# The residual of a down projection, joined after the first block instead of before it

## The chip, the cores and the metric

The kernel runs on one core of one Trainium2 chip. The metric is the device time of one execution in microseconds (us), as the median of three runs. The engines are named as in the profile: PE is TensorE (matmuls) and PEld its weight loads, DVE is VectorE, ACT is ScalarE, POOL is GpSimd, and SP is the engine whose queue issues the DMAs.

## The reference

One decoder layer: a mixer of two kinds of attention, cross-attention, and a multilayer perceptron, each added to a residual. Only the last part matters here. With x the residual of 1024 tokens by 1024 features:

```
u = relu(rmsnorm(x, ln2) @ w_ff1)        # 1024 -> 4096
x = x + (u * u) @ w_ff2                  # 4096 -> 1024: the down projection
return rmsnorm(x, ln_f)
```

All arithmetic is float32. The kernel writes each operand of a matmul as the sum of a rounded high part and the low rest, and takes three matmuls (low x high, high x low, high x high) for each product.

## The kernel before, in words

The activations lie with features on the 128 partitions and tokens along the free dimension, in two halves of 512 tokens.

**The recipe of seven.** Both projections of the perceptron are cut into blocks, and a block is a product of 2 x 2 by 2 x 2 sub-blocks done with seven products in place of eight (the Strassen-Winograd recipe). The inner dimension of 4096 makes eight blocks of 512 (`NB = 8`). Blocks 0 to 6 of the down projection use the recipe; block 7 is done plainly by `last_part` (L1559).

**The up projection** (the loop at L1422) works on 16 pairs `p_` of row tiles, two for each block. `Pair.run` (L1328) does one product of a pair (12 matmuls of 128x128 by 128x512) and evicts it. With a pair's last product (4) its results u11, u12, u21, u22 are complete, and `put_right` (blocks 0 to 6) or `put_plain` (L1393, block 7) makes a list of closures, `later`. Each closure writes tiles to DRAM with `put` (L1362): ACT copies a tile to its rounded high part in a small buffer (tags d and e), DVE makes the low part in place, and two DMAs of 256 KB write both. One closure is taken from `later` ahead of each product (L1433); what is left after the last product is run at L1441. Those are seven closures, all of `put_plain`, for block 7. Its order within a pair was u11, u21, u12, u22.

**The weights of the down projection.** `left(src)` (L1400) loads 512 KB of weights for one step into a buffer `wr` (two of these), lets POOL make four sums of quarters (L1410, tile z), and splits twice: the plain quarters into two tiles of the tag w4 (hq, lq: products 1, 2 and 4) and the sums into wh and wl (three buffers each: products 5, 6, 7 and 3). In the profile the high parts are ACT's line L132 and the low parts DVE's line L133. The tag w4 has five buffers. In the transition they are shared by hq and lq of the steps, by the tile that holds u22 of a pair, and by `by_norms`.

**The right operands** of a block are seven tiles of 1 MB (`rights`, L1446), loaded from DRAM into large tiles of the tag act. There are seven of these; four serve a block's right operands, and two are the running sums `x2`.

**The residual.** The kernel carries the down projection's sums divided by a norm factor for each token (`by_norms`, a row of 1024 repeated on all partitions, in a w4 buffer). The residual is in DRAM as `x2d`. Before, `x2_load(m)` (L1456) loads it for one of four row groups m, 1 MB, straight into the tile of the running sums; `scaled(m)` (L1469) multiplies it by `by_norms`, two DVE operations of 128x1024; and `distances` (L1475) lets POOL subtract the quarter x22 from x12 and x21. For, in the recipe, x12 and x21 are kept as their distance from x22, and `distances` with an addition at block 6 undoes it.

**The steps** (the loop at L1481) go over blocks b = 0 to 6 and, in each, row groups m = 0 to 3. A step asks for the next step's weights, then issues the loads that are to stand behind these in SP's queue (`issue_after`): the residual's next row group in the first three steps, and the next block's right operands in steps m = 2 and 3. Then come the seven products in the order 1, 5, 7, 6, 2, 4, 3, of six matmuls each. Products 2, 4 and 3 go on in the PSUM banks of products 1, 5 and 7. After each product a DVE operation adds the bank to a running sum or subtracts it (L1507): products 1, 5, 7 and 6 in turn to x22, then 2 to x11, 4 to x21 and 3 to x12. Products 2, 4 and 3 need the bank read before they begin.

**Order.** Each engine executes its queue in order. The kernel is written with a scheduler that places each engine's instructions by a timeline of its own, from the order of the program as a priority and from what is ready; so the order in the profile isn't quite that of the program. For example, products of step 1 whose weights were ready stand ahead of late products of step 0.

Of the kernel before, what the change touches and what calls it, by code (L numbers as in the profile page):

```python
# [11 lines left out]
AF = mybir.ActivationFunctionType  # L12
ALU = mybir.AluOpType
# [6 lines left out]
TH = 512  # L20
# [24 lines left out]
def hybrid_layer(ctx: ExitStack, tc: tile.TileContext, a: dict, out: bass.AP):  # L45
    nc = tc.nc
    v, s, g = nc.vector, nc.scalar, nc.gpsimd
# [11 lines left out]
    def sb(tag, shape, bufs, dt=F32):  # L59
        return pool.tile(shape, dt, tag=tag, name=name(tag), bufs=bufs)  # L60

    def act(dt=F32R):
        return sb("act", [P, 8, TH], 7, dt)
# [8 lines left out]
    def w4(shape=(P, 1024), dt=F32):  # L72
        t = sb("w4", [P, 1024], 5, dt)[: shape[0]]
        return t.rearrange("p (a b) -> p a b", b=shape[2]) if len(shape) == 3 else t
# [4 lines left out]
    def w2(tag, n=512, dt=F32, p=P):  # L79
        return sb("r_" + tag, [P, 512], BUFS[tag], dt)[:p, :n]  # L80
# [15 lines left out]
    def ov_():  # L96
        return ps_tile("ov")
# [13 lines left out]
    load = nc.sync.dma_start  # L111
# [70 lines left out]
    def mm3(ps, w, x, first, last, more=False):  # L182

        nc.tensor.matmul(ps, w[1], x[0], start=first, stop=False, skip_group_check=more)  # L184
        nc.tensor.matmul(ps, w[0], x[1], start=False, stop=False, skip_group_check=more)  # L185
        nc.tensor.matmul(ps, w[0], x[0], start=False, stop=last, skip_group_check=more)  # L186

    def both(pair, f):
        return f(pair[0]), f(pair[1])
# [76 lines left out]
    at = 0  # L266
# [33 lines left out]
    h = [(act(), act()), (act(), act())]  # L300
# [20 lines left out]
    for k in range(KT):  # L321
        if k == 2:
            load(wg_raw, a["w_gate"])
        if k % 2 == 0:
            c = slice(k % 4 * 256, k % 4 * 256 + 512)
# [93 lines left out]
    ps = ov_()  # L419
# [260 lines left out]
    for _ in range(2):  # L680
        t = act().rearrange("p a b -> p (a b)").rearrange("p (i c) -> p i c", i=4)
# [455 lines left out]
    x2d = dram.tile([P, KT // 2, 2, 2, TH], F32, name="x2d")  # L1137
# [23 lines left out]
    def bank():  # L1161
        turn[0] += 1
        return ps_tile(cycle[turn[0] % 8])

    def sub(out_, x, y, by=v):
        by.tensor_tensor(out=out_, in0=x, in1=y, op=ALU.subtract)
# [195 lines left out]
    def put(dst, x):  # L1362

        hi = rotate("d", "e").bitcast(F32R)
        split(hi, x.bitcast(F32R), x)
        load(dst[0], hi.bitcast(F32))
        load(dst[1], x)
# [24 lines left out]

    def put_plain(k, pair):  # L1393
        f = lambda i, hf: lambda: put([plain[2 * i + k, :, p_, hf] for p_ in range(2)], pair.u[f"{i + 1}{hf + 1}"])
        return [f(i, hf) for hf in range(2) for i in range(2)]


    after = [None]

    def left(src):  # L1400

        q = sb("wr", [P, 1024], 2)
        after[0] = load(q, src)
        q = q.rearrange("p (q c) -> p q c", q=4)
        q21, q11, q12, q22 = (q[:, i] for i in range(4))
        sums = z4()[:, :1024].rearrange("p (q c) -> p q c", q=4)
        s1, s2, s3, s4 = (sums[:, i] for i in range(4))

        for o, x, y, op in ((s1, q21, q22, ALU.add), (s2, s1, q11, ALU.subtract), (s3, q11, q21, ALU.subtract), (s4, s2, q12, ALU.subtract)):
            g.tensor_tensor(out=o, in0=x, in1=y, op=op)  # L1410
        hq, lq = (w4(dt=F32R)[:, :768].rearrange("p (q c) -> p q c", q=3) for _ in range(2))
        split(hq, lq, q[:, 1:])
        hs, ls = (sb(t, [P, 1024], 3, F32R).rearrange("p (q c) -> p q c", q=4) for t in ("wh", "wl"))
        split(hs, ls, sums)
        f = lambda hi, lo, i: both((hi, lo), lambda t: t[:, i].rearrange("p (k c) -> p k c", k=2))
        return {1: f(hq, lq, 0), 2: f(hq, lq, 1), 3: f(hs, ls, 3), 4: f(hq, lq, 2), 5: f(hs, ls, 0), 6: f(hs, ls, 1), 7: f(hs, ls, 2)}

    by_norms = w4()

    pairs = {}  # L1420
    later = []
    for at, (p_, i) in enumerate(jobs):  # L1422
        prepare(at)
        for _ in range(2 if at < 2 else 1):
            if rest and at:
                rest.pop(0)()
        if at == 6:
            norm_factors(1)
        if at == 30:
            to_row(by_norms, inv, 8, rowd[3:4], bank)  # L1430
        if at == len(jobs) - 3:
            lefts = left(a["w_ff2q"][0, 0])
        if later:  # L1433
            later.pop(0)()
        pair = pairs.setdefault(p_, Pair(p_))
        pair.run(i, cuts.pop((p_, i)))
        if i == 4:
            b, k = todo[p_][:2]
            later += put_right(b, k, pair) if b < NB - 1 else put_plain(k, pair)
            del pairs[p_]  # L1440
    for f in later:  # L1441
        f()

    SEVEN = (1, 5, 7, 6, 2, 4, 3)

    def rights(b, at):  # L1446

        t = act()
        n = min(2, 7 - at)
        for e in range(n):  # L1450
            load(t[:, 4 * e : 4 * e + 4].bitcast(F32), right[b][at + e].rearrange("p e k c -> p (e k) c"))
        return {SEVEN[at + e]: (t[:, 4 * e : 4 * e + 2], t[:, 4 * e + 2 : 4 * e + 4]) for e in range(n)}

    x2 = []

    def x2_load(m):  # L1456
        if m % 2 == 0:
            x2.append(act(F32).rearrange("p (m i h) c -> p m i h c", m=2, i=2))
        load(x2[m // 2][:, m % 2], x2d[:, m])

    steps = [(b, m) for b in range(NB - 1) for m in range(4)]
    r = {}
    r.update(rights(0, 0))
    r.update(rights(0, 2))
    x2_load(0)
    r.update(rights(0, 4))
    r.update(rights(0, 6))

    def scaled(m):  # L1469

        for i in range(2):
            x = x2[m // 2][:, m % 2, i].rearrange("p h c -> p (h c)")
            v.tensor_tensor(out=x, in0=x, in1=by_norms, op=ALU.mult)

    def distances(op, m):  # L1475

        x = x2[m // 2][:, m % 2]
        for i, hf in ((0, 1), (1, 0)):
            g.tensor_tensor(out=x[:, i, hf], in0=x[:, i, hf], in1=x[:, 1, 1], op=op)

    for at, (b, m) in enumerate(steps):  # L1481
        now = lefts
        if m == 0:
            r_now, r = r, {}
        if at + 1 < len(steps):
            b1, m1 = steps[at + 1]
            lefts = left(a["w_ff2q"][b1, m1])
        with tc.issue_after(after[0].ins):
            if at < 3:
                x2_load(at + 1)  # L1490
            if b + 1 < NB - 1:
                for i in ((), (), (0,), (2, 4, 6))[m]:
                    r.update(rights(b + 1, i))
        if at == 0:
            scaled(0)
            distances(ALU.subtract, 0)
        x = x2[m // 2][:, m % 2]
        x11, x12, x21, x22 = (x[:, i, j] for i in range(2) for j in range(2))
        held = {}

        for i, of, y, op in ((1, 1, x22, ALU.add), (5, 5, x22, ALU.add), (7, 7, x22, ALU.add), (6, 6, x22, ALU.add), (2, 1, x11, ALU.add), (4, 5, x21, ALU.subtract), (3, 7, x12, ALU.subtract)):
            if of == i:
                held[of] = bank()
            ps = held[of]
            for k in range(2):
                mm3(ps, both(now[i], lambda t: t[:, k]), both(r_now[i], lambda t: t[:, k]), of == i and k == 0, k == 1, True)
            v.tensor_tensor(out=y, in0=y, in1=ps, op=op)  # L1507
            if at < 3 and i == 5:
                scaled(at + 1)
                distances(ALU.subtract, at + 1)  # L1510
        if b == NB - 2:
            distances(ALU.add, m)


    us = []
    for i in range(2):
        t = act()
# [123 lines left out]
```

## Time and profile before

| | |
|---|---|
| median of three runs | 1542.23 us (1541.98 to 1542.44) |
| the profiled execution's own time | 1540.44 us |
| its span, from first to last instruction | 1538.7 us |
| granted TensorE clock, mean | 0.997 |
| down projection with the recipe | from about 1194 us, its last eviction starts at 1482.0 us |
| residual loads (L1459), four of 1 MB | issued from 1180.8 to 1215.0 us |
| scalings (L1473) | from 1189.4 to 1226.3 us |

Times within the profile are from the start of the span. A row of a group or of the timeline names the engine, the line, the operation, and "out<-in" by the program's tiles (the names of PSUM tiles are those of their tags: sc, tp, ov, and mm, m for the two single banks; tags such as r_d are the small buffers, wr, wh, wl, w and z those of the weights, with w for w4). "x" and a number is a count; "[idle before <-releaser]" tells how long the engine stood idle and whose end released it. A row of waits reads: who waited, for whom, in total us, how often, the longest.

### The profile page before, as it was taken

The page shows a single profiled execution, that of the slowest core. Times are in us where ns is not written, and L with a number is a line of the kernel's source. Part 1 is how long each engine was busy: PE and PEld are TensorE (multiplying, and loading weights), DVE is VectorE, ACT ScalarE, POOL GpSimd, SP SyncE. Part 2 cuts the span into 40 slices and gives each one's busy share as a digit, 9 for nine tenths or more (in the row PEclk, how much of TensorE's full clock was granted, in tenths as well). Part 3 has the DMA queues.
Part 4 walks back from the last instruction along what each step waited for, and adds up shares of the span by engine and source line. Part 5 has one row for each costly group of instructions (what it writes and reads, how often), then busy time and mean ns, then how long its engine had stood idle before and what let it go on. Part 6 is the DMA issues. An engine that isn't in the chain of part 4 may idle for free. (4 is left out here: it accounts for less than half of the span.)

```text
span 1538.7 us, 22030 instructions
## 1 busy us (share of the span) xinstructions
PE 1509.2 (98%) x7729; PEld 1259.7 (82%) x7729; DVE 1123.0 (73%) x1724; ACT 722.9 (47%) x1349; POOL 489.9 (32%) x527
## 2 busy tenths in 40 slices
PE   8999999999999999999999999999999999999997
PEld 8878888889898887788888877778787688888887
DVE  7656676665788875854457889898887987767665
ACT  7324343334688763543443466666664421111224
POOL 0002130414455441521110024544545543333322
PEclk9999999999999999999999999999999999999998
DMA  6422223436887958953444437776678966666623
GB/s 222 122 79 83 91 102 122 131 127 163 249 246 225 305 178 287 314 185 117 137 141 142 162 130 281 246 253 240 219 253 299 355 262 246 245 240 242 244 96 110
DMA packets 119803, 303.54 MB, mean 197 GB/s; under 512 B 13310, under 2 KB 27960, under 8 KB 111756
## 3 DMA queue, kind: packets, MB, share of 16 engines
q1 hardware_dynamic: 119692, 302.13, 57.7%
q8 instruction: 61, 1.00, 0.3%
q14 instruction: 50, 0.41, 0.1%
HBM read 202.22 MB, written 99.86 MB: 196 GB/s over the span
## 5 line engine op out<-in xcount | busy, mean ns | idle before, releaser
L184 PE MATMUL tp<-act,wl 128*128 128x512 f32 (+1 forms) x448 | 176.2, 393 | 1.4 <-ACT row L1339 0.7
L185 PE MATMUL tp<-act,wh 128*128 128x512 f32 (+1 forms) x448 | 175.3, 391 | 0.0
L186 PE MATMUL tp<-act,wh 128*128 128x512 f32 (+1 forms) x448 | 174.7, 391 | 0.0
L133 DVE TENSOR_TENSOR wl<-wr,wh 128x1024 fp32r<-128x1024 f32 (+2 forms) x99 | 129.5, 1309 | 23.7 <-ACT wh L132 23.4
L132 ACT ACTIVATE wh<-wr 128x1024 fp32r<-128x1024 f32 (+2 forms) x99 | 99.0, 1000 | 87.7 <-PE tp L186 34.6
L184 PE MATMUL mm<-act,wl 128*128 128x512 f32 (+1 forms) x336 | 130.6, 389 | 1.8 <-DVE r_c L518 0.9
L186 PE MATMUL mm<-act,wh 128*128 128x512 f32 (+1 forms) x336 | 129.0, 384 | 0.0
L185 PE MATMUL mm<-act,wh 128*128 128x512 f32 (+1 forms) x336 | 128.8, 383 | 0.0
L184 PE MATMUL m<-act,wl 128*128 128x512 f32 (+1 forms) x312 | 120.6, 386 | 2.0 <-POOL wl L947 1.6
L186 PE MATMUL m<-act,wh 128*128 128x512 f32 (+1 forms) x312 | 119.3, 382 | 0.0
L185 PE MATMUL m<-act,wh 128*128 128x512 f32 (+1 forms) x312 | 119.1, 382 | 0.0
L184 PEld LDWEIGHTS tp<-act,wl 128*128 128x128 f32 x448 | 84.2, 188 | 21.8 <-DVE wl L133 1.7
L1410 POOL TENSOR_TENSOR z<-wr 128x256 f32<-128x256 f32 x56 | 52.1, 950 | 152.1 <-DMA wr<-w_ff2q 139.2
L186 PEld LDWEIGHTS tp<-act,wh 128*128 128x128 f32 x448 | 84.2, 188 | 19.2
L185 PEld LDWEIGHTS tp<-act,wh 128*128 128x128 f32 x448 | 84.2, 188 | 18.8
L184 PE MATMUL sc<-act,wl 128*128 128x512 f32 (+1 forms) x248 | 97.0, 391 | 0.9 <-DVE wl L133 0.8
L185 PE MATMUL sc<-act,wh 128*128 128x512 f32 (+1 forms) x248 | 96.6, 390 | 0.0
L186 PE MATMUL sc<-act,wh 128*128 128x512 f32 (+1 forms) x248 | 96.6, 390 | 0.0
L132 ACT ACTIVATE w<-wr 128x768 fp32r<-128x768 f32 (+2 forms) x31 | 25.6, 824 | 145.3 <-PE tp L186 89.5
L132 ACT ACTIVATE wh<-z 128x1024 fp32r<-128x1024 f32 (+1 forms) x54 | 55.4, 1028 | 66.1 <-POOL z L1410 28.0
L133 DVE TENSOR_TENSOR wl<-z,wh 128x1024 fp32r<-128x1024 f32 (+1 forms) x54 | 75.1, 1391 | 3.4 <-ACT wh L132 3.3
L184 PEld LDWEIGHTS mm<-act,wl 128*128 128x128 f32 x336 | 63.3, 188 | 15.1 <-DVE r_c L518 1.2
(677 smaller groups left out, 4262.9 us busy)
## 6 DMA issues: line engine op xcount, KB each, us to landing
act<-right SPq DMA_DIRECT2D x49, 1024.0 KB
right<-w SPq DMA_DIRECT2D x56, 256.0 KB
wr<-w_ff2q SPq DMA_DIRECT2D x28, 512.0 KB
right<-r_d SPq DMA_DIRECT2D x49, 256.0 KB
right<-r_e SPq DMA_DIRECT2D x49, 256.0 KB
act<-fqk SPq DMA_DIRECT2D x48, 256.0 KB
wr<-w_in SPq DMA_DIRECT2D x20, 512.0 KB
wr<-w_ff SPq DMA_DIRECT2D x20, 512.0 KB
```

The source lines that it names most:

```text
L132: s.activation(hi, src, AF.Copy)
L133: return v.tensor_tensor(out=lo, in0=src, in1=hi.bitcast(F32), op=ALU.subtract)
L184: nc.tensor.matmul(ps, w[1], x[0], start=first, stop=False, skip_group_check=more)
L185: nc.tensor.matmul(ps, w[0], x[1], start=False, stop=False, skip_group_check=more)
L186: nc.tensor.matmul(ps, w[0], x[0], start=False, stop=last, skip_group_check=more)
L1410: g.tensor_tensor(out=o, in0=x, in1=y, op=op)
```

## The change

Four things are done.

1. **The first block's sums are copies.** In block 0 products 1, 2, 4 and 3 no longer add to a running sum that holds the residual. ACT copies the bank to the sum, times 1 or -1 (`s.activation(..., AF.Copy, scale=...)`). Products 5, 7 and 6 are added to x22 by DVE as before. The tile of the running sums is taken when a step of block 0 first needs it, not by a load.
2. **The residual joins in quarters in blocks 1 to 4.** In block b the residual of row group b - 1 is added, one quarter (128x512) per step, in the order x22, x12, x21, x11. A quarter is loaded (256 KB, in SP's queue behind the next step's weights) into a small buffer of the tag b or c (two of each); POOL multiplies it by half of `by_norms`; for x12 and x21 POOL also subtracts the quarter x22, which is kept; and DVE adds it to the running sum. `by_norms` is thereby needed until block 4 and not only in the first steps.
3. **The last plain tiles are split between products.** The seven closures that are left after the up projection are no longer run ahead of the down projection: one is taken from `later` in each product of the first steps, after its matmuls.
4. **Their order** within a pair is turned round: u22, u12, u21, u11.

```diff
     def put_plain(k, pair):
         f = lambda i, hf: lambda: put([plain[2 * i + k, :, p_, hf] for p_ in range(2)], pair.u[f"{i + 1}{hf + 1}"])
-        return [f(i, hf) for hf in range(2) for i in range(2)]
+        return [f(i, hf) for hf in (1, 0) for i in (1, 0)]
...
-    for f in later:
-        f()
-
...
-    def x2_load(m):
+    def sums_of(m):
         if m % 2 == 0:
             x2.append(act(F32).rearrange("p (m i h) c -> p m i h c", m=2, i=2))
-        load(x2[m // 2][:, m % 2], x2d[:, m])
+        return x2[m // 2][:, m % 2]
+
+    kept = {}
+
+    def residual(m, at):
+
+        i, hf = ((1, 1), (0, 1), (1, 0), (0, 0))[at]
+        t = w2("b" if at == 0 else "c")
+        with tc.issue_after(after[0].ins):
+            load(t, x2d[:, m, i, hf])
+        g.tensor_tensor(out=t, in0=t, in1=by_norms[:, hf * TH : hf * TH + TH], op=ALU.mult)
+        if at == 0:
+            kept[m] = t
+        elif at < 3:
+            sub(t, t, kept[m], g)
+        y = x2[m // 2][:, m % 2, i, hf]
+        v.tensor_tensor(out=y, in0=y, in1=t, op=ALU.add)
...
     r.update(rights(0, 2))
-    x2_load(0)
     r.update(rights(0, 4))
...
-    def scaled(m):
-
-        for i in range(2):
-            x = x2[m // 2][:, m % 2, i].rearrange("p h c -> p (h c)")
-            v.tensor_tensor(out=x, in0=x, in1=by_norms, op=ALU.mult)
-
-    def distances(op, m):
+    def joined(m):
 
         x = x2[m // 2][:, m % 2]
         for i, hf in ((0, 1), (1, 0)):
-            g.tensor_tensor(out=x[:, i, hf], in0=x[:, i, hf], in1=x[:, 1, 1], op=op)
+            g.tensor_tensor(out=x[:, i, hf], in0=x[:, i, hf], in1=x[:, 1, 1], op=ALU.add)
...
         with tc.issue_after(after[0].ins):
-            if at < 3:
-                x2_load(at + 1)
             if b + 1 < NB - 1:
                 for i in ((), (), (0,), (2, 4, 6))[m]:
                     r.update(rights(b + 1, i))
-        if at == 0:
-            scaled(0)
-            distances(ALU.subtract, 0)
-        x = x2[m // 2][:, m % 2]
+        x = sums_of(m) if b == 0 else x2[m // 2][:, m % 2]
+        if 0 < b < 5:
+            residual(b - 1, m)
...
-            v.tensor_tensor(out=y, in0=y, in1=ps, op=op)
-            if at < 3 and i == 5:
-                scaled(at + 1)
-                distances(ALU.subtract, at + 1)
+            if later:
+                later.pop(0)()
+            if b == 0 and i in (1, 2, 4, 3):
+                s.activation(y, ps, AF.Copy, scale=1.0 if op is ALU.add else -1.0)
+            else:
+                v.tensor_tensor(out=y, in0=y, in1=ps, op=op)
         if b == NB - 2:
-            distances(ALU.add, m)
+            joined(m)
```

## The prediction, made before the changed kernel was run

> **What bounds the kernel now.** I read the page first, then busy times by stretch, then whom TensorE waited for, then the order of the engines at those waits.
>
> ```profile
> span 1538.7 us, 22030 instructions
> ...
> PE 1509.2 (98%) x7729; PEld 1259.7 (82%) x7729; DVE 1123.0 (73%) x1724; ACT 722.9 (47%) x1349; POOL 489.9 (32%) x527
> ```
>
> TensorE (PE) is busy for 98% of the span, and the change takes no matmul away. So it can win back only gaps, some 30 us in all, and of these only those in the stretch that it edits. The stretches (TensorE, its weight loads, VectorE, ScalarE, GpSimd, the granted clock, DMA share, GB/s):
>
> ```profile
> core 0: us, PE busy (x) PEld busy (x) DVE busy (x) ACT busy (x) POOL busy (x), PEclk, DMA share, GB/s
> 1190.00:1240.00 50.00, 46.16 (x193) 35.36 (x192) 47.89 (x53) 20.08 (x29) 31.25 (x26) 1.00 0.93 332
> 1240.00:1280.00 40.00, 40.00 (x174) 32.20 (x173) 30.51 (x40) 9.76 (x11) 15.17 (x19) 1.00 0.60 230
> 1340.00:1390.00 50.00, 50.00 (x216) 40.30 (x215) 35.60 (x46) 9.92 (x11) 21.14 (x24) 1.00 0.52 200
> ```
>
> From 1190 to 1240 us, the end of the up projection and block 0 of the down projection, TensorE ran 193 matmuls; 50 us of the later blocks hold 216. The 23 missing ones, at 50/216 = 0.23 us, are 5.3 us. From 1240 on TensorE is full. In the gap VectorE is busy for 47.89 of 50 us and the DMA engines for 93%: VectorE is the suspect, DMA the second. TensorE's waits there (us, times, longest):
>
> ```profile
> PE m L184 <- DVE w L133: 1.2, 1, 1.2
> PE sc L184 <- DVE w L133: 0.8, 1, 0.8
> PE tp L184 <- DVE w L1326: 0.6, 1, 0.6
> PE mm L184 <- DVE wl L133: 0.6, 1, 0.6
> PE sc L184 <- DVE act L1507: 0.4, 1, 0.4
> PE tp L184 <- DVE wl L133: 0.2, 1, 0.2
> ```
>
> Six stalls, 3.8 us, each ended by VectorE. From 1240 to 1480 the same view has no row for TensorE. One stall in the timeline shows what it costs beyond its idle time:
>
> ```profile
> 1226.81 0.39 PE L186 MATMUL tp<-act,wh 128*128 128x512 f32 x1
> 1228.43 0.50 PE L184 MATMUL m<-act,w 128*128 128x512 f32 x1 [1.23 <-DVE w L133]
> 1228.77 0.39 PE L185 MATMUL m<-act,w 128*128 128x512 f32 x1
> ```
>
> From 1226.81 to 1228.77 are 1.96 us where two matmuls take 0.47: 1.49 us lost for 1.23 idle, so 0.26 more per stall. Six stalls lose 3.8 + 6 x 0.26 = 5.4 us, which agrees with the 5.3. **That is the ceiling of the gain.** VectorE's order around three of the stalls tells why it is late:
>
> ```profile
> 1215.05 2.35 DVE L1473 TENSOR_TENSOR act<-act,w 128x1024 f32<-128x1024 f32 x2
> 1217.32 0.67 DVE L1507 TENSOR_TENSOR act<-act,sc 128x512 f32<-128x512 f32 x1
> 1217.91 1.97 DVE L133 TENSOR_TENSOR wl<-z,wh 128x1024 fp32r<-128x1024 f32 x1
> ...
> 1225.15 2.35 DVE L1473 TENSOR_TENSOR act<-act,w 128x1024 f32<-128x1024 f32 x2
> 1227.43 0.95 DVE L133 TENSOR_TENSOR w<-wr,w 128x768 fp32r<-128x768 f32 x1
> ```
>
> The two scalings of the residual (L1473, 2.35 us) stand right ahead of the eviction, and ahead of the low half of the weights, that TensorE waits for.
>
> **The change part by part.** Durations (ns, min/median/max):
>
> ```profile
> L1473 DVE TENSOR_TENSOR act<-act,w x8: 1211/1396/2303, 1189.4 to 1226.3; 128x1024 f32<-128x1024 f32 x8
> L1507 DVE TENSOR_TENSOR act<-act,sc x70: 674/689/690, 1210.2 to 1477.4; 128x512 f32<-128x512 f32 x70
> L1479 POOL TENSOR_TENSOR act<-act x16: 1275/1300/2282, 1193.2 to 1482.8; 128x512 f32<-128x512 f32 x16
> L1339 ACT ACTIVATE r_p<-sc x4: 578/583/598, 982.5 to 1142.8; 128x512 f32<-128x512 f32 x4
> ```
>
> *Removed from the gap.* Eight scalings, 8 x 1.4 = 11 us of VectorE, and eight subtractions of GpSimd, 8 x 1.3 or more = 10 us. Sixteen of block 0's 28 evictions (products 1, 2, 4, 3 of four steps) go from VectorE to ScalarE: 16 x 0.69 = 11 us off VectorE, 16 x 0.58 = 9 us onto ScalarE, which has 30 of the 50 us free. VectorE falls from 47.9 to about 26 of 50 us. Four loads of 1 MB leave too; at 332 GB/s that is 3.2 us of all DMA engines each, 12.6 us together, out of a stretch that is 93% full.
>
> *The stalls that go with it*, each with its 0.26: the 1.23 and the 0.57 and the 0.23 (weights' low half behind scalings or late through the backlog), 0.41 (eviction behind a scaling), 0.60 (an eviction of the up projection, with scalings of steps 0 and 1 ahead of it): 3.04 + 5 x 0.26 = 4.3 us. The sixth, 0.8, is weights that came late because their buffers did, and is bounded by 0 and 1.06; the bigger weight tiles share a ring of five with by_norms and the last up-projection tiles:
>
> ```profile
> 1217.00 0.85 ACT L132 ACTIVATE w<-wr 128x768 fp32r<-128x768 f32 x1 [0.66 <-DMA plain<-w]
> ```
>
> Here ScalarE's part of a split waited until a last plain tile had been written out of such a buffer. The reversed order writes that tile (u22) first in its pair; but the second pair's is now the fourth of seven puts that are spread over step 0's products. I take half: 0.5. Sum 4.8 us.
>
> *The seven puts.* Seven copies of ScalarE, seven subtractions of VectorE and 14 writes of 256 KB are moved from ahead of step 0 to between its products, not added. On SP the writes go past the loads of step 1's weights, which gain by it; their own readers load after block 6, over 200 us later. So nothing, unless the buffers come later by it (in the 0.5 above). Nor do I count that the last right operands of block 0 are loaded earlier, since the sums now take their tile with the first copy and not with a load ahead of them: no stall waits on these operands.
>
> *Added, block 0.* The copy of product 1 stands in ScalarE's queue among the splits, and TensorE can't start product 2, in the same bank, before it. As written, products 5, 7, 6 lie between: 18 matmuls, 4.2 us. But at 1217 us only one product, 1.4 us, lay between. Rows for a full split:
>
> ```profile
> 1224.88 1.07 ACT L132 ACTIVATE wh<-z 128x1024 fp32r<-128x1024 f32 x1 [7.03 <-POOL z L1410]
> 1225.84 0.84 ACT L132 ACTIVATE w<-wr 128x768 fp32r<-128x768 f32 x1
> ```
>
> Two of these ahead of the copy: 1.91 + 0.58 - 1.40 + 0.26 = 1.35 us. Bounds: none, and one in each step, 5.4 us; if a split waits 7.03 us on GpSimd with copies behind it, more. I take one: 1.35 us, since the loads that made the splits late thin out.
>
> *Added, blocks 1 to 4.* Per block four loads of 256 KB, four multiplications and two subtractions on GpSimd (6 x 1.3 = 8 us), four additions on VectorE (4 x 0.69 at least, 2.8 us). The 1340 row has VectorE at 35.60 and GpSimd at 21.14 of 50 us; a block is 168 matmuls, 39.2 us, so 1.27 blocks lie in it, and they come to about 39 and 31. Adding 1 MB to a share of 0.52 to 0.6 costs no time by itself. by_norms stays in its buffer until block 4, so four buffers serve weights in place of five. A split then waits for TensorE's next release, and ScalarE waits so already:
>
> ```profile
> ACT w L132 <- PE tp L186: 89.5, 12, 9.6
> ```
>
> That is from 1240 to 1480, with no stall of TensorE: the splits run a step (42 x 0.233 = 9.8 us) ahead. I cost it at nothing; cover gone, it would be up to the 1.2 us of the first row above per step.
>
> What this cover doesn't reach is a VectorE that *waits* for a residual. Its additions stand in one queue with evictions. How late a load can land in the blocks:
>
> ```profile
> 1297.60 16.68 SPq L1403 DMA_DIRECT2D wr<-w_ff2q  x3
> 1302.00 2.80 POOL L1410 TENSOR_TENSOR z<-wr 128x256 f32<-128x256 f32 x2 [3.94 <-DMA wr<-w_ff2q]
> ...
> 1323.99 0.33 SPq L1403 DMA_DIRECT2D wr<-w_ff2q  x1
> 1333.03 1.43 POOL L1410 TENSOR_TENSOR z<-wr 128x256 f32<-128x256 f32 x2 [11.90 <-DMA wr<-w_ff2q]
> ```
>
> In a quiet time 4.4 us from issue to use, behind a burst of the next block's right operands 9.0. A quarter lands in such a burst once per block. If its addition was planned for 4.4 us, VectorE stands for 4.6 us, against a cover of 1.4 to 4.2: 0.7 to 3.5 us per block with the 0.26, bounds 0 and 14 us over four blocks. I take nothing: VectorE's addition has GpSimd's two operations ahead of it, and the plan already lives with such bursts without a stall.
>
> **Sum.** 4.8 - 1.35 = 3.45 us off. The profiled execution took 1540.44 us (span 1538.7): 1537.0. The median of the runs, 1542.23, lies 1.79 above it: **1538.8 us**.
>
> **A rule that speaks against it.** A VectorE operation with both inputs in SBUF is slowed beside GpSimd: the low half took 1.97 us at 1217.91, with GpSimd busy, and less beside an idle one:
>
> ```profile
> 1326.77 1.22 DVE L133 TENSOR_TENSOR wl<-z,wh 128x1024 fp32r<-128x1024 f32 x1
> ```
>
> Evictions from PSUM kept 0.67 to 0.69. The Trainium skill, "SBUF — State Buffer", section "Who interferes with whom", says that a VectorE instruction with two SBUF inputs contends with a GpSimd one that reads SBUF, on ports locked for a whole instruction. The trace agrees that only this kind is slowed. What it makes of the sum from rows is the third rival.
>
> **The rivals.**
> *Same (ScalarE becomes the late one):* the 1.35 us occurs in all four steps. 4.8 - 5.4: 0.6 us slower, 1542.8. For it: ScalarE's 7.03 us wait for GpSimd in the row above. Against: 30 free us, and GpSimd loses 10 us of work there. 0.14.
> *Same (buffers, not VectorE's load):* the two stalls on w (1.2 and 0.8) stay, since the slots come no earlier; 4.8 - 1.5 - 0.5 - 1.35 = 1.4 us off, 1540.8. For it: the row at 1217.00. Against: 2.35 us of scalings right ahead of the later one. Here the change does only half of what it says. 0.19.
> *Slower (a residual holds VectorE in the burst):* 3.5 us in each of four blocks, 14 - 3.45: 10.6 us slower, 1552.8. It decides from a wait above 1.4 us. For it: 9.0 us of landing. Against: the page's TensorE, full through every burst. 0.17, half of it with less than two blocks' worth.
> *Slower (shared ports):* if GpSimd's 8 us per block block VectorE in full, it is at 28 + 2.8 + 8 = 39 of 39.2 us (28 = 35.60/1.27), where 47.89 of 50 lost 5 us per 50. Four blocks, 16 us: 1554.8. Against: 1.97 - 1.22 = 0.75 us is all that one operation lost, 4.5 us per block, 35 of 39. 0.04.
>
> **How the numbers follow.** Forecast family (over 3.1 us off, 0.2%, about what a measurement of this kernel tells from no change) 0.46; the same 0.33; slower 0.21. The range: the low end is the ceiling, 5.4 off, 1536.8, less a little for the medians: 1536.5. The high end takes in both rivals without change and a burst stall in two blocks (7 - 3.45: 1545.8): 1546. About 0.04 lie below, 0.13 above.
>
> **What would show it.** Between 1190 and 1240 us VectorE near 26 of 50, TensorE over 48, and none of its waits on VectorE's act or wl left. Wrong if new rows name ACT act in TensorE's waits (first rival), if a wait on w stays (second), if VectorE waits for GpSimd in blocks 1 to 4 while TensorE shows gaps there (third), or if VectorE is over 37 of 40 in them (fourth).

## The result and the profile after

The changed kernel took 1535.99 us (median of five runs, 1535.26 to 1538.57) beside 1542.22 us (1541.95 to 1542.44) for the kernel before: a ratio of 0.9969, 95% interval 0.9958 to 0.998. Run again later, beside other executions of the kernel before, it took 1537.38 us (ten runs) against 1541.38 (thirteen): 0.9975, interval 0.9966 to 0.9985. So it is faster, by 6.2 us of the medians the first time and 4.0 the second.

The page of the changed kernel, span and busy times; below it the busy times by stretch, with the columns of the prediction's table:

```profile
span 1534.2 us, 22052 instructions
...
PE 1507.5 (98%) x7729; PEld 1262.1 (82%) x7729; DVE 1111.3 (72%) x1716; ACT 731.0 (48%) x1365; POOL 508.5 (33%) x543
```

```profile
1190.00:1240.00 50.00, 50.00 (x216) 40.37 (x215) 30.85 (x38) 28.91 (x44) 21.38 (x25) 1.00 0.79 295
1240.00:1280.00 40.00, 40.00 (x173) 32.30 (x172) 30.37 (x37) 9.10 (x11) 19.94 (x18) 1.00 0.65 252
1340.00:1390.00 50.00, 50.00 (x216) 40.34 (x215) 39.97 (x54) 11.34 (x12) 30.57 (x31) 1.00 0.60 224
```

TensorE is full from 1190 to 1240 us, 216 matmuls where there were 193, and the view of its waits has no row from 1180 to 1480. VectorE fell from 47.89 to 30.85 busy us, GpSimd from 31.25 to 21.38, the DMA share from 0.93 to 0.79; ScalarE rose from 20.08 to 28.91.

A total mixes this stretch with 1160 us of the program ahead of it, in which no instruction of an engine changed its order. For what follows I use two landmarks. One lies ahead of the change: the last start of ScalarE's copy to row from a bank sc. The other is the last start of an eviction of the blocks from a bank tp by VectorE. Both kernels, the kernel before first, then the changed one:

```profile
L1339 ACT ACTIVATE row<-sc x2: 580/582/585, 892.3 to 1161.2; 128x512 f32<-128x512 f32 x2
L1507 DVE TENSOR_TENSOR act<-act,tp x56: 673/686/690, 1209.0 to 1482.0; 128x512 f32<-128x512 f32 x56
```

```profile
L1339 ACT ACTIVATE row<-sc x2: 581/584/587, 893.8 to 1162.6; 128x512 f32<-128x512 f32 x2
L1515 DVE TENSOR_TENSOR act<-act,tp x52: 673/688/691, 1207.9 to 1477.9; 128x512 f32<-128x512 f32 x52
```

The changed stretch took 1482.0 - 1161.2 = 320.8 us before and 1477.9 - 1162.6 = 315.3 after: **5.5 us less**, the whole of what the six stalls cost. The changed kernel's other profile gives 1477.8 - 1162.5 = 315.3 too. The first landmark itself came 1.4 us later in the changed kernel's profile, though all ahead of it is the same: that is how far an unchanged part wanders, and why the totals spread by several us (28 executions of the kernel before, beside the first four experiments, took 1538.0 to 1543.8 us).

### The profile page after: what moved, and what is told of

The parts are those of the page before. It is cut to its first block, busy times and chain, and to the rows that moved or that the text cites. A ratio compares the mean times of both kernels' runs of the same rounds, so it can differ in the third digit from the quotient of the medians.

```text
span 1534.2 us, 22052 instructions
## 1 busy us (share of the span) xinstructions
PE 1507.5 (98%) x7729; PEld 1262.1 (82%) x7729; DVE 1111.3 (72%) x1716; ACT 731.0 (48%) x1365; POOL 508.5 (33%) x543
```

## The experiments

The theory behind the forecast: VectorE's queue makes the stalls, by its load or by the scalings that stand ahead of urgent work. The rivals: the DMA load, and the buffers of the last plain tiles. The first four experiments take the change apart, the others put the old work back piece by piece. The lost time of a run is its stretch less 315.3 us. Where old loads, scalings or subtractions are put back, their results are overwritten by block 0's copies, and the residual still joins in blocks 1 to 4; they cost time and change nothing that is computed.

**The plain tiles alone** (against the kernel before):

```diff
-        return [f(i, hf) for hf in range(2) for i in range(2)]
+        return [f(i, hf) for hf in (1, 0) for i in (1, 0)]
...
-    for f in later:
-        f()
...
+            if later:
+                later.pop(0)()
             v.tensor_tensor(out=y, in0=y, in1=ps, op=op)
```

> The kernel before with the plain tiles alone spread over the first products and in the new order (parts 3 and 4). TensorE's idle time from 1160 to 1480 us is 3.8 us in the kernel before and none in the changed one. If VectorE's scalings and evictions make the stalls, nearly all stay: 1541 to 1542.5 us, at most the 0.8 us stall gone. If the buffers that hold the last plain tiles make them, the two stalls on the weights' tile w (1.2 and 0.8 us, 2.5 us with restarts) go: about 1539.7 us. If the DMA load makes them, nothing goes: 1542.

1542.04 us, ratio 1.0004 (0.9996 to 1.0013); stretch 1485.9 - 1165.4 = 320.5. Its TensorE waits from 1170 to 1476 us:

```profile
PE sc L184 <- DVE w L133: 1.0, 1, 1.0
PE tp L184 <- DVE w L1326: 0.9, 1, 0.9
PE sc L184 <- DVE act L1506: 0.9, 1, 0.9
PE m L184 <- DVE act L1506: 0.8, 1, 0.8
PE tp L184 <- DVE wl L133: 0.2, 1, 0.2
```

Five stalls, 3.8 us in all, 5.1 with 0.26 for each restart. They moved, but parts 3 and 4 won nothing.

**The change without them** (against the changed kernel):

```diff
-        return [f(i, hf) for hf in (1, 0) for i in (1, 0)]
+        return [f(i, hf) for hf in range(2) for i in range(2)]
...
+    for f in later:
+        f()
...
-            if later:
-                later.pop(0)()
```

> The changed kernel with the plain tiles run ahead of block 0 in the former order (parts 1 and 2 alone). VectorE as the cause: 1536 to 1537 us, at most one stall of 0.8 us on the weights' tile w back. Buffers as the cause: the stalls of 1.2 and 0.8 us on w are back, about 1538.5 us. DMA load as the cause: 1536.

1536.88 us, ratio 0.9976 (0.9967 to 0.9985); stretch 1477.8 - 1162.5 = 315.3, no stall. The order and place of the plain tiles as a cause fall with these two: the gain is in parts 1 and 2 alone, and the sixth stall goes without parts 3 and 4.

**Copies on VectorE:**

```diff
-                s.activation(y, ps, AF.Copy, scale=1.0 if op is ALU.add else -1.0)
+                v.tensor_scalar(out=y, in0=ps, scalar1=1.0 if op is ALU.add else -1.0, scalar2=None, op0=ALU.mult)
```

> The changed kernel with the sixteen copies of block 0 on VectorE in place of ScalarE. VectorE goes from 30.9 to about 42 busy us of 50 between 1190 and 1240. If its total load makes the stalls, some are back: 1538 to 1540 us. If the pairs of scalings in front of evictions and weights make them, none or few are: 1536 to 1537. DMA load as the cause: 1536.

1537.06 us, ratio 0.9973 (0.9962 to 0.9984); stretch 1477.0 - 1161.7 = 315.3, no stall, with this row:

```profile
1190.00:1240.00 50.00, 50.00 (x216) 40.27 (x215) 38.73 (x52) 22.57 (x32) 16.22 (x19) 1.00 0.76 291
```

VectorE at 38.73 of 50 us stalls nothing here. That the copies went to ScalarE was not needed for the gain.

**The 1 MB loads back**, into the tiles of the sums:

```diff
-    def sums_of(m):
+    def x2_load(m):
         if m % 2 == 0:
             x2.append(act(F32).rearrange("p (m i h) c -> p m i h c", m=2, i=2))
-        return x2[m // 2][:, m % 2]
+        load(x2[m // 2][:, m % 2], x2d[:, m])
...
     r.update(rights(0, 2))
+    x2_load(0)
...
+            if at < 3:
+                x2_load(at + 1)
...
-        x = sums_of(m) if b == 0 else x2[m // 2][:, m % 2]
+        x = x2[m // 2][:, m % 2]
```

> The changed kernel with the four residual loads of 1 MB back at their former places in SP's queue, into the tiles of the sums, which block 0's copies overwrite; the residual still joins in blocks 1 to 4. 4 MB more are moved in the gap. VectorE as the cause: 1536 to 1537 us, no stall in the gap. DMA load as the cause: the stalls are back, 1540 us or more.

1538.15 us, ratio 0.9981 (0.9972 to 0.999); stretch 1478.5 - 1162.2 = 316.3, 1.0 lost. Its first stretch, its one stall, and ScalarE's order ahead of it:

```profile
1190.00:1240.00 50.00, 49.31 (x212) 39.40 (x211) 26.63 (x35) 29.32 (x45) 16.31 (x20) 1.00 0.97 366
```

```profile
PE m L184 <- ACT act L1516: 0.7, 1, 0.7
```

```profile
1207.43 0.63 ACT L132 ACTIVATE r_d<-w 128x512 fp32r<-128x512 f32 x1 [0.64 <-DMA plain<-r_d]
1208.78 0.85 ACT L132 ACTIVATE w<-wr 128x768 fp32r<-128x768 f32 x1 [0.72 <-DMA plain<-w]
1209.70 0.60 ACT L1516 ACTIVATE act<-m 128x512 f32<-128x512 f32 x1
```

The DMA engines are 97% busy, fuller than in the kernel before, and none of the old stalls is back: DMA load by itself is not their cause. The one stall, which was not expected here, is new, and it is the first rival's mechanism at work: product 1's copy stands in ScalarE's queue behind splits that wait 0.64 and 0.72 us for writes to land, and TensorE waits 0.69 for it.

**The scalings back as well** (further to the loads):

```diff
+    def scaled(m):
+        for i in range(2):
+            x = x2[m // 2][:, m % 2, i].rearrange("p h c -> p (h c)")
+            v.tensor_tensor(out=x, in0=x, in1=by_norms, op=ALU.mult)
...
+        if at == 0:
+            scaled(0)
...
+            if at < 3 and i == 5:
+                scaled(at + 1)
```

> The changed kernel with the four loads of 1 MB and VectorE's eight scalings of 128x1024 back at their former places; block 0's copies overwrite what they make, and the residual still joins in blocks 1 to 4. Measured by the changed stretch, from the last start of ScalarE's copy to row from a bank sc (L1339) to the last start of an eviction of the blocks by VectorE: 320.8 us in the kernel before, 315.3 in the changed one, 316.3 with the loads alone back. VectorE comes to about 39 busy us of 50 between 1190 and 1240, as with the copies on VectorE, which had no stall. If the place of the scalings ahead of urgent work makes the stalls, rows with VectorE's act, w or wl are back and the stretch is 318 to 320 us. If VectorE's total load makes them, the stretch stays near 316.3.

1538.81 us, ratio 0.9984 (0.9975 to 0.9994); stretch 1480.5 - 1163.5 = 317.0, 1.7 lost:

```profile
PE m L184 <- ACT act L1524: 0.7, 1, 0.7
PE tp L184 <- DVE wl L133: 0.5, 1, 0.5
```

```profile
1190.00:1240.00 50.00, 49.31 (x212) 39.48 (x211) 37.69 (x44) 27.06 (x43) 19.65 (x21) 1.00 0.96 366
```

One stall of 0.5 us on VectorE, 0.76 with the restart, at a load that did no harm with the copies. So the place of the scalings counts, or the loads beside them, which the kernel with VectorE's copies did not have; but for an eighth of the old loss. The stretch lies between what place and load were each expected to give.

**Scalings and VectorE's copies** (both edits above):

> The same as the one with the scalings back, with block 0's sixteen copies on VectorE too: nearly VectorE's work of the kernel before, about 46 busy us of 50, while GpSimd's eight subtractions stay away. Both place and load expect stalls on VectorE: a stretch of 319 to 321 us. If GpSimd's subtractions are needed for the stalls, by slowing VectorE's operations from SBUF, it stays under 318 us.

1539.60 us, ratio 0.9988 (0.9978 to 0.9997); stretch 1481.6 - 1163.7 = 317.9, 2.6 lost. The expectation that place or load would bring all back failed; it came out in the other branch, under 318:

```profile
PE sc L184 <- DVE act L1524: 1.0, 1, 1.0
PE m L184 <- DVE act L1524: 0.8, 1, 0.8
```

```profile
1190.00:1240.00 50.00, 48.18 (x205) 37.93 (x204) 43.33 (x55) 20.23 (x30) 19.77 (x22) 1.00 0.97 362
```

**And GpSimd's subtractions**, all the old work:

```diff
+    def distances(m):
+        x = x2[m // 2][:, m % 2]
+        for i, hf in ((0, 1), (1, 0)):
+            sub(x[:, i, hf], x[:, i, hf], x[:, 1, 1], g)
...
             scaled(0)
+            distances(0)
...
                 scaled(at + 1)
+                distances(at + 1)
```

> The kernel with loads, scalings and vector copies back, and GpSimd's eight subtractions of 128x512 back too: all the work of the kernel before stands in the gap again (its results are overwritten, and the residual still joins later). The changed stretch was 317.9 us without the subtractions and 320.8 in the kernel before. If GpSimd's subtractions are the missing part (by delaying the sums of the weights, z, and slowing VectorE's operations from SBUF), the stretch is 320 to 321.5 us. If they are not, and the rest lies in the residual's place in the chain of sums, it stays near 318 us.

1541.88 us (one run); stretch 1483.7 - 1162.9 = 320.8, 5.5 lost, as in the kernel before:

```profile
PE sc L184 <- DVE w L133: 1.1, 1, 1.1
PE sc L184 <- DVE act L1531: 1.0, 1, 1.0
PE tp L184 <- DVE w L1326: 0.9, 1, 0.9
PE m L184 <- DVE act L1531: 0.8, 1, 0.8
PE tp L184 <- DVE wl L133: 0.2, 1, 0.2
```

```profile
1190.00:1240.00 50.00, 45.93 (x193) 35.42 (x192) 46.93 (x51) 18.59 (x28) 32.88 (x28) 1.00 0.92 337
```

The subtractions, on an engine off the path, added the last 2.9 of the 5.5 us: with them VectorE is at 46.93 us, where 43.33 was the load without. Its operations on two SBUF tiles from 1190 to 1240 us (busy us, mean ns), first without the subtractions, then with them:

```profile
L1486 DVE TENSOR_TENSOR act<-act,w 128x1024 f32<-128x1024 f32 x8 | 10.5, 1351 | 0.0
L133 DVE TENSOR_TENSOR wl<-z,wh 128x1024 fp32r<-128x1024 f32 x4 | 5.1, 1276 | 1.7 <-ACT wh L132 1.7
```

```profile
L1486 DVE TENSOR_TENSOR act<-act,w 128x1024 f32<-128x1024 f32 x8 | 12.4, 1592 | 0.3 <-DMA act<-x2d 0.3
L133 DVE TENSOR_TENSOR wl<-z,wh 128x1024 fp32r<-128x1024 f32 x4 | 7.2, 1809 | 0.0
```

The same twelve operations took 4.0 us longer. No run puts the work of VectorE and GpSimd back without the loads of 1 MB, so what these add to it stays open.

**Subtractions without scalings** (`distances` added to the kernel with the loads back):

> The changed kernel with the four loads of 1 MB and GpSimd's eight subtractions back at their former places, without the scalings; block 0's copies overwrite the results. With the loads alone the stretch was 316.3 us. If the subtractions alone delay the weights' sums enough, 317 to 319 us with TensorE waiting on wl. If they need a VectorE that is full as well, 316 to 316.8.

1537.15 us (one run); stretch 1479.2 - 1162.7 = 316.5: 0.2 us over the loads alone, and the copy's stall stays the only one. Its first stretch:

```profile
1190.00:1240.00 50.00, 49.31 (x211) 39.07 (x210) 28.49 (x35) 28.09 (x44) 31.05 (x29) 1.00 0.99 375
```

**Subtractions with scalings, copies on ScalarE:**

> The changed kernel with loads, scalings and subtractions back, the copies of block 0 on ScalarE as in the change. The scalings alone gave 317.0 us. If the subtractions add what was missing whatever engine evicts, 319.5 to 320.5 us; if only a VectorE that also evicts is hurt by them, 317 to 318.

1537.31 us (one run); stretch 1479.4 - 1161.3 = 318.1, 2.8 lost:

```profile
PE m L184 <- ACT act L1531: 0.7, 1, 0.7
PE tp L184 <- DVE w L1326: 0.7, 1, 0.7
PE tp L184 <- DVE wl L133: 0.4, 1, 0.4
```

```profile
1190.00:1240.00 50.00, 48.57 (x207) 38.33 (x206) 39.91 (x42) 26.78 (x44) 32.14 (x27) 1.00 0.98 370
```

The subtractions added 0.2 us to the loads alone, 1.1 beside the scalings and 2.9 where VectorE also evicts: they hurt only beside a VectorE that has much to do.

**The quarters behind the burst** (the rival that was to end slower):

```diff
+    behind = [None]
...
-            load(t[:, 4 * e : 4 * e + 4].bitcast(F32), right[b][at + e].rearrange("p e k c -> p (e k) c"))
+            behind[0] = load(t[:, 4 * e : 4 * e + 4].bitcast(F32), right[b][at + e].rearrange("p e k c -> p (e k) c"))
...
-        with tc.issue_after(after[0].ins):
+        with tc.issue_after(behind[0].ins):
             load(t, x2d[:, m, i, hf])
...
-        if 0 < b < 5:
-            residual(b - 1, m)
...
+        if 0 < b < 5 and m == 3:
+            for q_ in range(4):
+                residual(b - 1, q_)
```

> The changed kernel with all four quarters of a residual joined after the last step of a block, their loads in SP's queue behind the next block's right operands, the latest place there is. If a VectorE that waits for a late quarter holds up evictions (the rival of the prediction), TensorE stalls by 0.7 to 3.5 us per block: a stretch of 318 to 329 us. If VectorE's place in the plan moves back with the loads, or its queue has room, it waits less than 1.4 us each time and the stretch stays at 315 to 316 us.

1538.17 us, ratio 0.9979 (0.997 to 0.9988); stretch 1479.2 - 1162.3 = 316.9, 1.6 lost. One stretch and its one stall, in the timeline:

```profile
1300.00:1350.00 50.00, 48.95 (x210) 38.85 (x209) 43.12 (x53) 10.62 (x11) 34.60 (x33) 1.00 0.63 230
```

```profile
1301.11 1.22 DVE L1474 TENSOR_TENSOR act<-act,r_c 128x512 f32<-128x512 f32 x1 [0.57 <-POOL r_c L1166]
...
1303.04 1.41 DVE L133 TENSOR_TENSOR w<-wr,w 128x768 fp32r<-128x768 f32 x1
...
1304.51 0.50 PE L184 MATMUL sc<-act,w 128*128 128x512 f32 x1 [0.97 <-DVE w L133]
...
1306.24 0.19 PEld L184 LDWEIGHTS mm<-act,wl 128*128 128x128 f32 x1 [0.51 <-DVE wl L133]
1306.24 0.50 PE L184 MATMUL mm<-act,wl 128*128 128x512 f32 x1
```

This is neither of the two stretches that were expected. VectorE waited for a quarter four times, 0.6 us at most. The longest of these waits, 0.57 us, stands shortly ahead of the low half that TensorE waits for, so it can be a part of the stall; the rest is a VectorE that does a block's four additions, GpSimd's work beside them, in one step. The stall and its restart are 1.2 of the 1.6 us. The other 0.3 are the late weights at 1306.24: that matmul starts 0.47 us after the one before it and the next 0.34 after it, where 0.23 is usual.

**The residual's arithmetic on VectorE:**

```diff
-        g.tensor_tensor(out=t, in0=t, in1=by_norms[:, hf * TH : hf * TH + TH], op=ALU.mult)
+        v.tensor_tensor(out=t, in0=t, in1=by_norms[:, hf * TH : hf * TH + TH], op=ALU.mult)
...
-            sub(t, t, kept[m], g)
+            sub(t, t, kept[m])
```

> The changed kernel with the residual's multiplications and subtractions in blocks 1 to 4 on VectorE in place of GpSimd: six operations of 0.69 us or more per block. VectorE goes from 39.5 to about 45 busy us of 50 between 1300 and 1350. If a load of over 40 of 50 is what makes stalls, they appear in blocks 1 to 4: a stretch of 317 to 320 us. If spread short operations do no harm, it stays at 315 to 316 us.

1537.30 us, ratio 0.9972 (0.9961 to 0.9983); stretch 1478.8 - 1163.4 = 315.4, no stall:

```profile
1300.00:1350.00 50.00, 50.00 (x216) 40.29 (x215) 43.70 (x61) 8.71 (x9) 23.36 (x23) 1.00 0.59 226
```

In the blocks VectorE at 43.70 of 50 us stalls nothing, where 43.12 did with the four additions in one step. That the weights are cut a step ahead there is the likely reason; no run tests it.

**The change again:**

> The changed kernel once more, unaltered, to see how far one program repeats: every theory expects a stretch of 315.2 to 315.4 us without a stall, and a total within 1535 to 1538.5 us, since what differs lies ahead of the stretch.

1537.38 us (1535.38 to 1538.34), stretch 315.3, no stall, as expected. No kernel here beats the changed one in the stretch: at 315.3 us TensorE has no gap left in it. The five profiles without a stall, of four kernels, come to 315.3 or 315.4; each kernel with stalls has one profile, so how far these repeat is not known.

## Why the prediction was right, and where it was off

*The ceiling* was 5.4 us, from two estimates; the stretch lost 5.5. The stall view and the count of matmuls were enough to tell it. That VectorE's queue made the stalls was right too.

*The forecast* was 3.45 us off, 1538.8 us. The two medians are 1535.99 and 1537.38; the first lies 0.5 us below the low end of the range. Two terms of the sum were mis-sized. The step that took one wait of the copies in ScalarE's queue at 1.35 us: no such wait occurred in the changed kernel. The mechanism is real, as the loads put back show (0.69 us and its restart), but it came only in kernels with the loads that the change took away. And the step that took half of the sixth stall for buffers: all of it went, without parts 3 and 4 too. Without the 1.35 and with the 0.5 more the sum is 4.8 + 0.5 = 5.3. What the totals show above or below 5.5 lies outside the stretch, in code that is the same; so it says little that the second median lies inside the range and the first below it.

*The row at 1217.00*, ScalarE waiting for a plain tile's write, was read as a sign that buffers make a stall. It was a wait of an engine with room. Undone and done alone, the order of the tiles moved 0.0 and 0.3 us.

*VectorE late by the scalings right ahead of it*: shown in part. Put back on top of the loads, the scalings cost 0.7 us, and 1.6 with the subtractions there, not 4. The loss followed the sum of VectorE's work. Lost time beside VectorE's busy us of 50, in the kernels with the loads in the gap, less the 1.0 of the copy's stall where it occurs: 26.6 none, 28.5 0.2, 37.7 0.7, 39.9 1.8, 43.3 2.6, 46.9 5.5. The scheduler orders each kernel anew, so these are not one order with pieces added.

*GpSimd's subtractions* were costed as 10 us off an engine with room. Put back last they were worth 2.9 us, through VectorE, whose operations they lengthen. That isn't a price of their own: a piece cost more, the more was there already. The subtractions cost 0.2 us on top of the loads alone; VectorE's copies cost 2.7 on top of all the rest, 0.9 without the subtractions (both with ScalarE's stall of 1.0 gone) and none by themselves. The low halves that VectorE makes from two SBUF tiles, from 1180 to 1240 us, in the kernel before and in the changed one:

```profile
L133 DVE TENSOR_TENSOR wl<-z,wh 128x1024 fp32r<-128x1024 f32 x4 | 7.4, 1840 | 0.0
```

```profile
L133 DVE TENSOR_TENSOR wl<-z,wh 128x1024 fp32r<-128x1024 f32 x6 | 7.7, 1290 | 5.3 <-ACT wh L132 5.3
```

1.84 us fell to 1.29 each. VectorE also made six of them in place of four, in nearly the same time: it works ahead now. It is at 30.85 us and not at the forecast 26 for another reason. The forecast took 16 evictions out of the window from 1190 to 1240 us; but 24 evictions (L1507) had stood in it and 13 (L1515) stand there now, so only 11 went, some 3.4 us less, and an addition of a quarter, 1.2 us, came in. The Trainium skill, "SBUF — State Buffer", section "Who interferes with whom", has the rule: two SBUF inputs on VectorE contend with GpSimd's reads. The prediction weighed it against the change, for blocks 1 to 4. The runs agree with the rule, and show it working for the change, in the gap: the low halves and scalings above took longer with the subtractions back.

*Shared ports in the blocks:* VectorE's additions of a quarter are slowed, but TensorE did not notice. Their durations in the changed kernel, and with the arithmetic on VectorE:

```profile
L1472 DVE TENSOR_TENSOR act<-act,r_c x12: 679/1188/1395, 1257.4 to 1380.0; 128x512 f32<-128x512 f32 x12
```

```profile
L1472 DVE TENSOR_TENSOR act<-act,r_c x12: 677/682/1222, 1257.8 to 1386.6; 128x512 f32<-128x512 f32 x12
```

From 1340 to 1390 us VectorE came to 39.97 where 39 was forecast, and GpSimd to 30.57 where 31 was.

*The late quarter* was priced at up to 14 us. In the changed kernel VectorE waits for quarters, but briefly (1240 to 1400 us):

```profile
DVE act L1472 <- POOL r_c L1166: 3.2, 3, 1.5
DVE act L1472 <- POOL r_b L1466: 0.7, 1, 0.7
```

Its longest, 1.5 us, was above the point of 1.4 from which it was to decide, and stalled nothing; with all quarters put behind the whole burst, 1.6 us were lost, not 14. The step that failed is the price, a VectorE that stands for 4.6 us: with the latest loads the longest wait was 0.6.

## What to carry to other kernels

Where TensorE waits in one stretch only, add up the work of the engine it waits for in that stretch, and move what need not be there to stretches where that engine stalls nothing. Where VectorE works on two SBUF tiles, count as its load also what GpSimd does beside it: taking work from GpSimd can be a part of what frees VectorE. Put pieces back in more than one order before giving each its price. For an effect of a few us in 1540, compare two landmarks around the changed code rather than totals.

## What the runs showed of the hardware that was not expected

Lost time did not grow in proportion to VectorE's load: from 1190 to 1240 us, without the copy's stall, it was at most 0.7 us up to 38.7 of 50, 1.8 at 39.9, 2.6 at 43.3 and 5.5 at 46.9; in the blocks, 43.7 cost nothing, but 43.1 with the additions in one step cost 1.6. And the same instructions in the same order reached the first landmark at 1161.2 to 1165.4 us over these 14 profiles, a spread near the size of the effect.
